# Two-layer GLA and Mamba-2 trunk on one core: squares and gate rows at the start, root and stores at the end, given to other engines and memories

## The chip, the core and the metric

One NeuronCore of a Trainium2 chip. Its engines run side by side and meet at semaphores: TensorE (PE; its weight loads are shown as PEld), VectorE (DVE), ScalarE (ACT), GpSimd (POOL), and SyncE (SP), which here only issues DMAs. The metric is the device time of one execution in microseconds (us); lower is better.

## The reference

The input `x` has 1024 tokens of width 1024, all in float32. Two layers, each with a residual:

```python
for i in range(2):
    hn = rmsnorm(x, norm_w[i])
    x = x + (gla_mixer if i % 2 == 0 else ssd_mixer)(hn, ...)
return rmsnorm(x, final_norm)

def rmsnorm(x, w):
    return x * rsqrt(mean(x * x, -1) + 1e-6) * w
```

The GLA mixer projects `hn` to q, k, v, a gate g and a low-rank decay input `gk_low` (16 columns), runs a chunked recurrence for 4 heads, normalizes each head, multiplies with silu(g) and projects back. The Mamba-2 mixer projects to z, x, B, C and dt, runs a short convolution, a chunked scan for 32 heads in 8 groups, a gated norm, and projects back.

## The kernel before

Activations lie feature-major: eight blocks of 128 features (`KB`) on the partitions, tokens along the free dimension in two tiles of `T = 512`. The four stages in time are GLA on token tile 0, GLA on tile 1, Mamba-2 on tile 0, Mamba-2 on tile 1. float32 products run as three products of rounded parts (`mm3`, lines 223 to 225): high times high, low times high, high times low. So each operand has a high part (`hh`, `wh`, a rounded copy by ScalarE) and a low part (`hl`, `wl`, the difference, by VectorE or GpSimd).

Weights come through a list of `units`. `prefetch` (lines 161 to 188) keeps `RAWS = 3` raw loads and `SPLIT = 4` split weights ahead: the load on SP's queue, line 171 the rounded copy on ScalarE, line 176 the low part on GpSimd. `run` goes through the units and lets generators (the mixers, norms and loads) take steps beside them. The order of the instructions on each engine is not the one in which they are written: a planner in the build puts them in order by readiness in its own model of time and by priority. Exceptions are instructions wrapped in `VP`, `AP_`, `GP` (`InOrder`, line 391), which stay behind everything that was written before them on their engine.

**The start.** `load_acc` brings the eight blocks of `x` into `accs`. `raw_rows` (line 362) makes, for each block k, `hh` = x times the norm weight, rounded (line 370, ScalarE), and `hl` (line 371, VectorE), then squares x (`square_into`, lines 315 to 321: ScalarE into a tile of the pool `t`, VectorE adds it to `ss`). The norm's factor isn't in these rows: the root is made later and multiplied into the results. When the sum `ss` is complete, lines 377 to 388 sum it over partitions on TensorE (lines 379 and 381), take Ln and Exp on ScalarE, and one Newton step on VectorE (`newton`, lines 308 to 313). The first results, q, k and one block of g in three of the four PSUM banks `pp`, can be evicted only with this root (lines 444 and 419). The v products (lines 469 to 471) take all four banks `pp`, so they wait for these evictions. After v comes the small projection `gk` (`small_units`, line 245): its right-hand rows are rebuilt from `hh` + `hl` at line 260, even blocks on VectorE, odd ones on GpSimd, and its matmuls are at line 268. The pool `t` has eight tiles, and PSUM has four banks `pp` and four `mb`.

**The end.** The last output projection of Mamba-2 on tile 1 is done in two halves of 256 tokens, `outp_half(0)` and `outp_half(1)` (line 1120 on): eight blocks of 12 matmuls each; each block is evicted into `accs` by VectorE, squared by ScalarE, and the squares of the second half are added by GpSimd. `final_half(hf)` (line 1162) sums the squares over partitions (line 1168), makes the root (`v`, Ln, Exp, `newton`), scales the eight blocks and stores them in four DMAs of two blocks each. `final_half(0)` runs step by step beside the matmuls of `outp_half(1)`; `final_half(1)` runs alone after the last matmul. Most of these instructions go through the wrapper at line 398, so the rows of the profile name that line.

Of the kernel before, what the change touches and what calls it, by code (L numbers as in the profile page):

```python
# [13 lines left out]
AF = mybir.ActivationFunctionType  # L14
ALU = mybir.AluOpType
# [5 lines left out]
KB = D // P  # L21
# [18 lines left out]
C_NORM = 0  # L40
C_FIN = C_NORM + 16
# [12 lines left out]
def hybrid_kernel(ctx: ExitStack, tc: tile.TileContext, xT, w_in0, w_gk, w_up, w_out0,  # L54
                  w_in1, w_dt, w_out1, par, masks, tri, out):
    nc = tc.nc
    V, A, G, PE = nc.vector, nc.scalar, nc.gpsimd, nc.tensor
    dma = nc.sync.dma_start
# [12 lines left out]
    def tl(tag, bufs, shape=(P, T), dt=F32):  # L71
        cnt[0] += 1
        return sb.tile(list(shape), dt, name=f"{tag}_{cnt[0]}", tag=tag, bufs=bufs)

    def ps(tag):
        cnt[0] += 1
        return (psp if tag == "pp" else psm).tile([P, T], F32, name=f"{tag}_{cnt[0]}", tag=tag)

    def tmp(n=P):
        t = tl("t", NTMP)  # L80
        return t[:] if n == P else t[0:n, :]

    def c3(ap, w=P):
        return ap.rearrange("p (n w) -> p n w", w=w)
# [5 lines left out]
    def act(out, in_, func, **k):  # L90
        name = SILU if func == AF.Silu else LN_EXP
        i = None
        if name != table[0]:
            i = A.preload_act_table_set(name)
            for m in table[2]:
                tc.add_manual_dep(i.ins, m.ins.name, ORDER, reason="table")
            table[:] = name, i, []
        o = A.activation(out, in_, func, **k)
        tc.add_manual_dep(o.ins, table[1].ins.name, ORDER, reason="table")
        table[2].append(o)  # L100
        return o
# [32 lines left out]
    def col(c, n=P):  # L134
        return pr[0:n, c:c + 1]
# [76 lines left out]
    def drain(g):  # L212
        for _ in g:
            pass
# [27 lines left out]

        return [(piece(*src, hf), T, half(hf)) for hf in range(2)]

    def small_units(src, rh, rl, evac):

        box, first = [], len(units)  # L250

        def half(hf):
            def prep():
                if hf == 0:
                    box.append(tl("w2", 1, (P, KB, 32)))
                    A.copy(box[0][:], c3(raws[first][:, 0:KB * 32], 32))
                rows = []
                for k in range(4 * hf, 4 * hf + 4):
                    rows.append(tmp())
                    (G if k % 2 else V).tensor_tensor(rows[-1], rh[k].bitcast(F32), rl[k].bitcast(F32), op=ALU.add)  # L260
                return rows

            def f(*rows):
                if hf == 0:
                    box.append(ps("pp"))
                w, o = box
                for j in range(4):
                    PE.matmul(o[32 * j:32 * (j + 1), :], w[:, 4 * hf + j, :], rows[j], start=(hf == 0), stop=(hf == 1))
                if hf == 1:
                    def sums():  # L270
                        a = tmp(32)
                        A.copy(a, o[0:32, :])
                        for j in range(1, 4):
                            V.tensor_tensor(a, o[32 * j:32 * (j + 1), :], a, op=ALU.add)
                        evac(a)
                    pend.append(sums)
            return f, prep

        for hf in range(2):
            f, prep = half(hf)  # L280
            units.append((None if hf else (src, None), KB * 32, f, None, prep))
# [15 lines left out]
    def rstd_of(p, n, box, var, stay=False):  # L297
        v = tmp() if var is None else var
        V.tensor_scalar(v, p[:], 1.0 / n, EPS, op0=ALU.mult, op1=ALU.add)
        r = p[:] if stay else tl("rstd", 3)[:]  # L300
        l = tmp()
        act(l, v, AF.Ln)
        act(l, l, AF.Exp, scale=-0.5)
        newton(V, r, v, l)
        box.append(r)
        yield

    def newton(eng, r, v, l):

        m = tmp()[:, 0:v.shape[1]]  # L310
        eng.tensor_tensor(m, v, l, op=ALU.mult)
        eng.scalar_tensor_tensor(m, m, -0.5, l, op0=ALU.mult, op1=ALU.mult)
        eng.scalar_tensor_tensor(r, m, 1.5, l, op0=ALU.add, op1=ALU.mult)

    def square_into(ss, src, first, eng):
        if first:
            A.activation(ss, src, AF.Square)
        else:
            sq = tmp()
            A.activation(sq, src, AF.Square)  # L320
            eng.tensor_tensor(ss, ss, sq, op=ALU.add)  # L321
# [38 lines left out]
    accs = {}  # L360

    def raw_rows(rh, rl, r):

        ss = tl("ss", 3)[:]
        for k in range(KB):
            x = accs[k]
            w = col(C_NORM + k)
            a = tl(f"hh{k}", 1, dt=F32R)[:]
            b = tl(f"hl{k}", 1, dt=F32R)[:]
            A.mul(a, x, w)  # L370
            V.scalar_tensor_tensor(b, x, w, a.bitcast(F32), op0=ALU.mult, op1=ALU.subtract)  # L371
            rh.append(a)
            rl.append(b)
            yield
            square_into(ss, x, k == 0, V)
            yield
        with tc.high_priority():
            p, q = ps("mb"), ps("mb")
            PE.matmul(p[:], ones[:], ss, start=True, stop=True)
            for c in range(NC):  # L380
                PE.matmul(q[:, c:c + 1], ss[:, c * P:(c + 1) * P], one, start=True, stop=True)
            drain(rstd_of(p, D, r, None))
            rt = cst.tile([P, 3, NC], F32, name="rtok")
            V.tensor_scalar(rt[:, 0, :], q[:, 0:NC], 1.0 / D, EPS, op0=ALU.mult, op1=ALU.add)
            act(rt[:, 1, :], rt[:, 0, :], AF.Ln)
            act(rt[:, 1, :], rt[:, 1, :], AF.Exp, scale=-0.5)
            newton(V, rt[:, 2, :], rt[:, 0, :], rt[:, 1, :])
        r.append(rt[:, 2, :])
        yield
# [10 lines left out]
    VP, AP_, GP = InOrder(V), InOrder(A), InOrder(G)  # L400


    def load_acc(t):
        for k in range(KB):
            accs[k] = tl(f"acc{k}", 1)[:]
            dma(accs[k], xsrc(0, k, t))
            yield

    class Gla:
# [13 lines left out]
        def gk(self):  # L423
            def evac(o):

                low = o
                if self.raw:
                    V.tensor_tensor(low, o, self.r[0][0:32, :], op=ALU.mult)
                st = tl("stp", 2, (P, T), F32R)
                G.memset(st[96:P, :].bitcast(F32), 0.0)  # L430
                V.tensor_copy(st[0:32, :], low)
                V.tensor_tensor(st[32:64, :], low, st[0:32, :].bitcast(F32), op=ALU.subtract)
                V.tensor_copy(st[64:96, :], low)
                self.low = st[:]
            small_units(w_gk, self.rh, self.rl, evac)

        def qkv(self, h):
            base = h * 10
# [313 lines left out]
    class Ssd:  # L752
# [409 lines left out]
        def final_half(self, hf):  # L1162
            if hf == 0:
                yield
            ts = slice(hf * 256, (hf + 1) * 256)
            p = ps("mb")[:, 0:256]
            for i in (0, KB - 2, KB - 1) if hf else (0, KB - 1):
                PE.matmul(p, ones[:], self.sq[hf][i], start=(i == 0), stop=(i == KB - 1))
            ot = [c3(tl(*(("wh", 5) if hf else ("v", 6)))[:], 256) for _ in range(4)]
            o = [ot[fb // 2][:, fb % 2, :] for fb in range(KB)]  # L1170
            dst = out[:, :, self.t * T + hf * 256:self.t * T + (hf + 1) * 256].rearrange("f p w -> p f w")
            for fb in range(5, KB):
                AP_.mul(o[fb], accs[fb][:, ts], col(C_FIN + fb))
            yield
            v, r, l = tmp()[:, 0:256], tl("rstd", 3)[:, 0:256], tmp()[:, 0:256]
            VP.scalar_tensor_tensor(v, p, 1.0 / D, self.var[:, ts], op0=ALU.mult, op1=ALU.add)
            tc.keep_in_program_order(act(l, v, AF.Ln))
            tc.keep_in_program_order(act(l, l, AF.Exp, scale=-0.5))
            yield
            newton(VP, r, v, l)  # L1180
            yield
            for fb in range(5, KB):
                GP.tensor_tensor(o[fb], o[fb], r, op=ALU.mult)
            for fb in range(5):
                VP.scalar_tensor_tensor(o[fb], accs[fb][:, ts], col(C_FIN + fb), r, op0=ALU.mult, op1=ALU.mult)
                if fb == 1:
                    yield
            for i in range(4):
                dma(dst[:, 2 * i:2 * i + 2, :], ot[i])


    ph = [Gla(0), Gla(1), Ssd(0), Ssd(1)]
# [46 lines left out]
    for p in range(2):  # L1239
        g = ph[p]  # L1240
        for h in range(GH):
            o = [lambda: g.outp(h - 1)] if h else ([lambda: ph[0].outp(3)] if p else [])
# [52 lines left out]
    xs, rows = load_acc(0), raw_rows(ph[0].rh, ph[0].rl, ph[0].r)  # L1295
# [109 lines left out]
```

## Time and profile before

| | us |
|---|---|
| median of 3 runs | 1612.12 (1608.9 to 1615.64) |
| profiled execution, device time | 1609.57 |
| its span, first to last instruction | 1607.8 |
| TensorE busy in the span | 1570.2 (98%) |
| VectorE / ScalarE / GpSimd busy | 951.4 / 951.4 / 655.3 |

The profile is of one execution. A row of a view names an engine, a source line and the tiles in the form written<-read. "waits" are idle stretches of an engine, put down to the instruction that ended last before the engine went on. The chain of waits starts at the last instruction of the span and follows back what released each step. The granted clock is TensorE's, as a share of its full speed.

### The profile page before, as it was taken

To read this page: it belongs to the slowest core of one execution; us is meant where nothing else is said; L and a number is where in the kernel's file an instruction comes from. 1 tells how busy PE (TensorE), PEld (TensorE's weight loads), DVE (VectorE), ACT (ScalarE), POOL (GpSimd) and SP (SyncE) were. 2 spreads that over 40 slices of the span, in tenths; PEclk is the share of its full clock that TensorE was granted. 3 is DMA by queue.
4 is the path that set the end of the run, shared out by engine and by line. 5 is a ranking of instruction groups with operands and counts; after the bars stand their busy time and mean duration, and the time that the engine had idled before them with its cause. 6 is when DMAs were issued, how large, how long until landed. Compare 5 with 4: busy or idle time off the path is not lost.

```text
span 1607.8 us, 24028 instructions
## 1 busy us (share of the span) xinstructions
PE 1570.2 (98%) x8272; PEld 1305.0 (81%) x8272; DVE 951.4 (59%) x1579; ACT 951.4 (59%) x1796; POOL 655.3 (41%) x542
## 2 busy tenths in 40 slices
PE   7999899999999999999999999999999999999996
PEld 5787787878888888888888888888778888888886
DVE  6357567495725446386735544457976963355657
ACT  4445363544636264564865767656657777667743
POOL 6456565643411021216536656565523222222322
PEclk9999999999999999999999999999999999999999
DMA  7545465464576456464586565566665766655752
GB/s 235 194 146 156 137 195 190 132 220 161 183 268 197 151 191 202 154 200 146 174 276 202 179 199 184 181 193 222 226 198 193 240 238 217 206 177 188 259 199 85
DMA packets 172747, 309.30 MB, mean 192 GB/s; under 512 B 19089, under 2 KB 25105, under 8 KB 172625
## 3 DMA queue, kind: packets, MB, share of 16 engines
q1 hardware_dynamic: 172624, 307.77, 58.6%
q8 instruction: 65, 1.06, 0.3%
q14 instruction: 58, 0.47, 0.1%
HBM read 232.06 MB, written 75.63 MB: 191 GB/s over the span
## 4 chain that ended last, share of the span: by engine, by line
PE 78%; DVE 11%; DMA 4%; ACT 4%; issue 1%; POOL 1%; SPq 0%; DVEq 0%; ACTq 0%; POOLq 0%
PE pp L223 18%; PE pp L224 18%; PE pp L225 18%; PE pp L469 3%; PE pp L470 3%; PE pp L471 3%; DMA wraw<-w_in 2%; PE mb L956 2%; PE mb L709 2%; PE mb L708 2%; PE mb L658 1%; PE mb L949 1%; DVE o L604 1%; PE mb L223 1%; PE mb L224 1%
## 5 line engine op out<-in xcount | busy, mean ns | idle before, releaser
L171 ACT CAST wh<-wraw 128x512 fp32r<-128x512 f32 x472 | 289.4, 618 | 343.1 <-PE pp L224 164.3
L223 PE MATMUL pp<-hh,wh 128*128 128x512 f32 x1184 | 468.5, 397 | 8.8 <-ACT wh L171 7.4
L224 PE MATMUL pp<-hl,wh 128*128 128x512 f32 x1184 | 464.0, 392 | 1.3 <-DVE hl L371 1.1
L225 PE MATMUL pp<-hh,wl 128*128 128x512 f32 x1184 | 463.0, 392 | 0.0
L176 POOL TENSOR_TENSOR wl<-wraw,wh 128x512 fp32r<-128x512 f32 x240 | 328.3, 1375 | 277.1 <-ACT wh L171 232.3
L223 PEld LDWEIGHTS pp<-hh,wh 128*128 128x128 f32 x1184 | 222.8, 188 | 60.3 <-ACT wh L171 9.0
L224 PEld LDWEIGHTS pp<-hl,wh 128*128 128x128 f32 x1184 | 223.0, 188 | 48.5 <-DVE hl L371 2.5
L225 PEld LDWEIGHTS pp<-hh,wl 128*128 128x128 f32 x1184 | 222.9, 188 | 46.2
L223 PE MATMUL pp<-yh,wh 128*128 128x512 f32 x448 | 177.9, 397 | 6.1 <-DVE acc L515 5.4
L225 PE MATMUL pp<-yh,wl 128*128 128x512 f32 x448 | 175.9, 393 | 0.0
L224 PE MATMUL pp<-yl,wh 128*128 128x512 f32 x448 | 175.4, 392 | 0.0
L321 POOL TENSOR_TENSOR ss<-ss,t 128x512 f32<-128x512 f32 x53 | 74.0, 1396 | 81.8 <-ACT t L320 70.4
L223 PEld LDWEIGHTS pp<-yh,wh 128*128 128x128 f32 x448 | 84.2, 188 | 26.1 <-issue 2.8
L469 PE MATMUL pp<-wh,hh 128*128 128x512 f32 x256 | 100.4, 394 | 2.7 <-DVE m L444 2.7
L470 PE MATMUL pp<-wl,hh 128*128 128x512 f32 x256 | 100.3, 392 | 0.0
L471 PE MATMUL pp<-wh,hl 128*128 128x512 f32 x256 | 99.7, 392 | 0.0
L225 PEld LDWEIGHTS pp<-yh,wl 128*128 128x128 f32 x448 | 84.3, 188 | 18.9 <-issue 0.2
L224 PEld LDWEIGHTS pp<-yl,wh 128*128 128x128 f32 x448 | 84.2, 188 | 17.8
L827 DVE SCALAR_TENSOR_TENSOR m<-pp,pr,m 128x509 f32<-128x509 f32 (+2 forms) x96 | 70.4, 743 | 42.8 <-ACT m L824 41.7
L827 DVE SCALAR_TENSOR_TENSOR x<-pp,pr,x 128x509 f32<-128x509 f32 (+2 forms) x96 | 71.2, 743 | 32.5 <-ACT x L824 31.4
L648 POOL TENSOR_TENSOR t<-v,t 128x512 fp32r<-128x512 f32 x28 | 38.1, 1371 | 112.6 <-DMA wraw<-w_in 28.9
L1038 POOL TENSOR_TENSOR t<-t,o 128x512 fp32r<-128x512 f32 x32 | 41.8, 1310 | 91.6 <-ACT o L1036 87.0
(286 smaller groups left out, 2623.7 us busy)
## 6 DMA issues: line engine op xcount, KB each, us to landing
wraw<-w_in SPq DMA_DIRECT2D x352, 256.0 KB, 3.5
low_in<-wl SPq DMA_DIRECT2D x176, 256.0 KB, 3.8
wl<-low_in SPq DMA_DIRECT2D x176, 256.0 KB, 3.2
wraw<-w_out SPq DMA_DIRECT2D x128, 256.0 KB, 3.5
low_out<-wl SPq DMA_DIRECT2D x64, 256.0 KB, 4.0
v<-a_cum SPq DMA_DIRECT2D x64, 256.0 KB, 3.8
wl<-low_out SPq DMA_DIRECT2D x56, 256.0 KB, 3.2
xn<-x SPq DMA_DIRECT2D x43, 256.0 KB, 3.8
```

What stands on the lines that cost most here:

```text
L171: A.copy(hi[:, 0:w], raws[n][:, 0:w])
L176: G.tensor_tensor(lo[:, 0:w], raws[n][:, 0:w], hi[:, 0:w].bitcast(F32), op=ALU.subtract)
L223: PE.matmul(o, lh, rh, start=first, stop=False)
L224: PE.matmul(o, lh, rl, start=False, stop=False)
L225: PE.matmul(o, ll, rh, start=False, stop=last)
L321: eng.tensor_tensor(ss, ss, sq, op=ALU.add)
L469: PE.matmul(o, rh[kb][:, cs], wh[:], start=(kb == 0), stop=False)
L470: PE.matmul(o, rh[kb][:, cs], wl[:], start=False, stop=False)
L471: PE.matmul(o, rl[kb][:, cs], wh[:], start=False, stop=(kb == KB - 1))
L648: G.tensor_tensor(vl, v[c], vh.bitcast(F32), op=ALU.subtract)
L827: V.scalar_tensor_tensor(dst[:, s:], o[:, 0:T - s], col(C_CW + j * 32 + si), dst[:, s:], op0=ALU.mult, op1=ALU.add)
L1038: G.tensor_tensor(xel[-1], xe, hi.bitcast(F32), op=ALU.subtract)
```

## The change

- In `raw_rows` the square of block 0 is pinned in ScalarE's order behind what was written before it; those of blocks 1 to 7 go to a PSUM bank of the tag `mb` instead of a tile of the pool `t`, and VectorE adds them from there.
- In `small_units`, for the first GLA stage only, the eight rows are made by ScalarE as `accs[k]` times the norm weight instead of by VectorE and GpSimd as `hh` + `hl`.
- In `final_half` the result of the Newton step stays in the PSUM bank `p` of the sum. ScalarE copies it to SBUF for GpSimd. GpSimd scales blocks 6 and 7 (ScalarE multiplies their column factor in ahead) instead of 5 to 7, and VectorE scales 0 to 5, reading the root from PSUM.
- In the second half, the stores of the pairs 1 and 3 are issued from ScalarE's queue, those of 0 and 2 from SP's.

```diff
--- before.py
+++ after.py
@@ -242,7 +242,7 @@
 
         return [(piece(*src, hf), T, half(hf)) for hf in range(2)]
 
-    def small_units(src, rh, rl, evac):
+    def small_units(src, rh, rl, evac, again=None):
 
 
 
@@ -257,6 +257,9 @@
                 rows = []
                 for k in range(4 * hf, 4 * hf + 4):
                     rows.append(tmp())
+                    if again:
+                        again(k, rows[-1])
+                        continue
                     (G if k % 2 else V).tensor_tensor(rows[-1], rh[k].bitcast(F32), rl[k].bitcast(F32), op=ALU.add)
                 return rows
 
@@ -372,7 +375,13 @@
             rh.append(a)
             rl.append(b)
             yield
-            square_into(ss, x, k == 0, V)
+            if k == 0:
+
+                AP_.activation(ss, x, AF.Square)
+            else:
+                sq = ps("mb")[:]
+                A.activation(sq, x, AF.Square)
+                V.tensor_tensor(ss, sq, ss, op=ALU.add)
             yield
         with tc.high_priority():
             p, q = ps("mb"), ps("mb")
@@ -432,7 +441,8 @@
                 V.tensor_tensor(st[32:64, :], low, st[0:32, :].bitcast(F32), op=ALU.subtract)
                 V.tensor_copy(st[64:96, :], low)
                 self.low = st[:]
-            small_units(w_gk, self.rh, self.rl, evac)
+            small_units(w_gk, self.rh, self.rl, evac,
+                        (lambda k, row: A.mul(row, accs[k], col(C_NORM + k))) if self.raw else None)
 
         def qkv(self, h):
             base = h * 10
@@ -1169,24 +1179,26 @@
             ot = [c3(tl(*(("wh", 5) if hf else ("v", 6)))[:], 256) for _ in range(4)]
             o = [ot[fb // 2][:, fb % 2, :] for fb in range(KB)]
             dst = out[:, :, self.t * T + hf * 256:self.t * T + (hf + 1) * 256].rearrange("f p w -> p f w")
-            for fb in range(5, KB):
+            for fb in range(6, KB):
                 AP_.mul(o[fb], accs[fb][:, ts], col(C_FIN + fb))
             yield
+
             v, r, l = tmp()[:, 0:256], tl("rstd", 3)[:, 0:256], tmp()[:, 0:256]
             VP.scalar_tensor_tensor(v, p, 1.0 / D, self.var[:, ts], op0=ALU.mult, op1=ALU.add)
             tc.keep_in_program_order(act(l, v, AF.Ln))
             tc.keep_in_program_order(act(l, l, AF.Exp, scale=-0.5))
             yield
-            newton(VP, r, v, l)
-            yield
-            for fb in range(5, KB):
+            newton(VP, p, v, l)
+            yield
+            AP_.copy(r, p)
+            for fb in range(6, KB):
                 GP.tensor_tensor(o[fb], o[fb], r, op=ALU.mult)
-            for fb in range(5):
-                VP.scalar_tensor_tensor(o[fb], accs[fb][:, ts], col(C_FIN + fb), r, op0=ALU.mult, op1=ALU.mult)
+            for fb in range(6):
+                VP.scalar_tensor_tensor(o[fb], accs[fb][:, ts], col(C_FIN + fb), p, op0=ALU.mult, op1=ALU.mult)
                 if fb == 1:
                     yield
             for i in range(4):
-                dma(dst[:, 2 * i:2 * i + 2, :], ot[i])
+                (AP_.dma_start if hf and i % 2 else dma)(dst[:, 2 * i:2 * i + 2, :], ot[i])
 
 
     ph = [Gla(0), Gla(1), Ssd(0), Ssd(1)]
```

## Rows read from the trace of the kernel before

**Rows 1.** The page: busy us, share of the span, instructions.
```profile
PE 1570.2 (98%) x8272; PEld 1305.0 (81%) x8272; DVE 951.4 (59%) x1579; ACT 951.4 (59%) x1796; POOL 655.3 (41%) x542
```

**Rows 2.** Windows: length, busy (count) PE, PEld, DVE, ACT, POOL; clock, DMA share, GB/s.
```profile
23.66:32.75 9.09, 9.09 (x41) 7.22 (x40) 8.16 (x11) 3.26 (x7) 8.07 (x6) 1.00 0.72 226
32.75:35.43 2.68, 0.00 (x2) 0.00 (x1) 2.68 (x6) 0.12 (x1) 1.38 (x2) 1.00 0.85 287
35.43:40.50 5.07, 5.07 (x15) 4.04 (x16) 1.74 (x3) 0.50 (x1) 3.88 (x4) 0.66 0.30 99
```

**Rows 3.** Waits, 0 to 60 us: total us, times, longest.
```profile
PE pp L469 <- DVE m L444: 2.7, 1, 2.7
...
PE mb L379 <- DVE ss L321: 0.5, 1, 0.5
```

**Rows 4.** Chain of waits, 0 to 62 us: start, us, what.
```profile
20.06 1.77 DVE ss L321
...
29.39 2.30 DVE t L260 x2
...
32.30 1.68 DVE t L260
...
34.72 0.66 DVE m L444
```

**Rows 5.** Timeline, GpSimd, 19 to 60 us: start, us, instruction.
```profile
24.81 2.55 POOL L260 TENSOR_TENSOR t<-hh,hl 128x512 f32<-128x512 f32 x2
```

**Rows 6.** Single lines: ns min/median/max, first and last start.
```profile
L321 DVE TENSOR_TENSOR ss<-ss,t x35: 672/692/1793, 10.4 to 1265.9; 128x512 f32<-128x512 f32 x35
...
L889 DVE TENSOR_TENSOR acc<-pp,acc x40: 672/683/693, 1023.6 to 1575.2; 128x512 f32<-128x512 f32 x40
```

**Rows 7.** Groups by form, ScalarE: busy us, mean ns, idle before.
```profile
L722 ACT COPY o<-mb 128x256 f32<-128x256 f32 x32 | 12.0, 374 | 45.0 <-PE mb L709 45.0
...
L370 ACT ACTIVATE hh<-acc,pr 128x512 fp32r<-128x512 f32 x8 | 5.7, 714 | 2.2 <-DMA acc<-xT 2.2
...
L553 ACT COPY mb<-m 128x512 f32<-128x512 f32 x8 | 4.7, 591 | 8.3 <-DVE m L551 8.3
```

**Rows 8.** Chain of waits, 1594 to 1608 us.
```profile
1594.82 0.73 POOL ss L398
...
1595.60 1.58 PE mb L1168 x6
```

**Rows 9.** Timeline, 1585 to 1608 us, of single engines.
```profile
1584.96 0.59 PE L1168 MATMUL mb<-ss,ones 128*128 128x256 f32 x2
...
1589.35 0.74 POOL L398 TENSOR_TENSOR v<-v,rstd 128x256 f32<-128x256 f32 x1 [0.43 <-DVE rstd L398]
...
1590.90 0.28 PE L225 MATMUL mb<-ktok,hl 128*128 128x256 f32 x1
...
1591.51 2.38 DVE L398 SCALAR_TENSOR_TENSOR v<-acc,pr,rstd 128x256 f32<-128x256 f32 x3
...
1593.73 0.28 PE L225 MATMUL mb<-ktok,hl 128*128 128x256 f32 x1
...
1594.48 0.41 DVE L398 TENSOR_TENSOR acc<-mb,acc 128x256 f32<-128x256 f32 x1
...
1600.01 3.47 DVE L398 SCALAR_TENSOR_TENSOR wh<-acc,pr,rstd 128x256 f32<-128x256 f32 x5
```

**Rows 10.** Stores: SP's issues; DMA busy tenths and GB/s, 1601 to 1607.8, 40 slices.
```profile
1603.11 0.89 SPq L1189 DMA_DIRECT2D out<-wh  x2
...
1604.09 0.45 SPq L1189 DMA_DIRECT2D out<-wh  x1
...
DMA  0000000399991000029999999999999300000000
GB/s 0 0 0 0 0 0 0 120 361 337 355 319 48 0 0 0 0 78 331 319 349 374 320 313 379 343 350 331 355 355 319 109 0 0 0 0 0 0 0 0
```

**Rows 11.** Windows, behind the start (columns as in rows 2).
```profile
57.50:200.00 142.50, 136.42 (x750) 113.25 (x750) 89.54 (x167) 66.84 (x124) 77.43 (x61) 1.00 0.48 151
```

## Prediction

> **What bounds the kernel now.** I read the page first: TensorE is busy 1570.2 of 1607.8 us [rows 1], so everything between the two ends is a full TensorE, and a change at the ends can win only the 37.6 us in which it stands still. [...] The view of waits names the causes: 2.7 us for the eviction `m` (line 444), 0.5 us for the sum of squares `ss` (line 321) [rows 3]. The chain of waits then shows what made these late. The last add into `ss` took 1.77 us, and ahead of the eviction at 34.72 VectorE spent 2.30 and 1.68 us on line 260, the adds that rebuild the rows for the small gate projection [rows 4], which nobody needs before 57 us. While VectorE waited there, GpSimd ran its own half of these adds and the weight splits [rows 5].
>
> At the other end the last product starts at 1593.73, and from there to 1607.8 runs one serial chain: the late eviction, squares, GpSimd's last add, six matmuls of the cross-partition sum, root, scaling, stores [rows 8, 9]. After the last issue (1604.09) three stores are still in flight back to back at some 340 GB/s with the DMA engines over 90% busy [rows 10].
>
> **The start, part by part.** *Squares in PSUM.* Seven adds `ss` keep their place and count; one operand now comes from PSUM. With two SBUF operands this add takes 672 ns at best and 1793 at worst; with a PSUM operand the same shape took 672 to 693 in all 40 cases [rows 6], though GpSimd is busy for 41% of the span [rows 1]. So the last add falls from 1.77 to 0.69, 1.1 us sooner. TensorE gets only the part in which it stood: 0.5 us [rows 3], since its queue is full up to there. The last `hl` (line 371, two SBUF operands) keeps its collision with GpSimd, so the gap ahead of it stays. ScalarE's square into PSUM is not in the trace; the nearest row is a copy of the same shape into PSUM, 591 ns [rows 7], so I take 0.6, unchanged. The four banks `mb` turn over fast enough: the fifth square needs the bank of the first, whose add is by then over 2 us old.
>
> [...]
>
> *First square pinned.* It moves behind the first weight cast on ScalarE; the first product could start some 0.5 us sooner. That is lost later in the wait for the last `hl`: zero. If it doesn't come, nothing is lost either. A clock that rises sooner would be a gain that I don't count.
>
> *Rows by ScalarE.* Four adds leave VectorE and four leave GpSimd (2.55 us for one pair [rows 5]); eight scalings of a 128x512 tile come to ScalarE, at 714 ns each by line 370, the same form: 5.7 us. ScalarE is busy only 3.26 of 9.09 us from 23.66 to 32.75, 0.12 of 2.68 and 0.50 of 5.07 behind that [rows 2], so they fit there; what waits behind them in its queue are weight casts, which run several units ahead. Ahead of the eviction 4.0 us of VectorE's work go (2.30 and 1.68 [rows 4]), plus the 0.5 from `ss`: the eviction starts near 30.2 and ends near 30.9, while TensorE would run out of banks at 32.75 less 0.5. The 2.68 us go entirely, with 1.3 us to spare. What is late next is the eviction of the third bank, two operations of 0.7 us behind: it just fits.
>
> *The clock.* The stretch of 5.07 us at 0.66 lost 0.34 x 5.07 = 1.7 us, right after the gap. Without the gap I count this as won.
>
> Sum at the start: 0.5 + 2.7 + 1.7 = 4.9. Against it: three of the eight row tiles may be free from the beginning (no square draws from their pool any more), and their scalings need only the input. A planner could put them ahead of the first operands on ScalarE, where there is little room. Each costs 0.71; three are 2.1, and the lower end is zero, if they fall into ScalarE's waits for weights. I take 0.4, nearer to zero, since the other five have the room of the windows. Start: **4.5**, between 1.5 and 5.5. From 57 us on TensorE is the limit again and the 4.5 us stay.
>
> **The end, part by part.** *VectorE's backlog.* In the first half's scaling three operations took 2.38 us (0.79 each), so the evictions of blocks 5 to 7 queued up and the last began at 1594.48, though the products of block 5 were done at 1591.2 and those of block 7 at 1594.0 [rows 9]. The root now lies in PSUM; the eviction with a PSUM operand in the same rows takes 0.41, and I take 0.43 with the column factor. The four scalings that stand behind the eviction of block 4 then take 1.7 us instead of three in 2.4. The last eviction follows its product at 1594.1 instead of 1594.48: 0.4 us. More is won in the sum: block 5's square and GpSimd's add (0.73, ended at 1595.55 [rows 8]) now end near 1594.1, so the first four of the six matmuls (1.58 us in all [rows 8]) run while the last square is made. Only two, 0.59 us [rows 9], stand behind it: 1594.1 + 0.41 + 0.45 + 0.05 + 0.59 gives 1595.6 instead of 1597.17: **1.55**.
>
> The copy of the root for GpSimd is new: ScalarE, PSUM to SBUF at 128x256, 374 ns [rows 7]. In the first half it waits for the root, and behind it in the queue is the square of block 4, whose eviction comes later anyway. GpSimd starts 0.4 to 0.8 us later but has two products instead of three (0.74 each uncontended), and its last add still ends at about 1594.1: cover just complete. If it fails, each 0.1 us late there is 0.1 at the end.
>
> *The last scaling and the stores.* Root to last scaling was 3.47 us for five operations, 0.69 each instead of some 0.43 [rows 9], beside three products of GpSimd. Six at 0.44 are 2.6. GpSimd's two end at 0.45 + 2 x 0.74 = 1.95 after the root, ahead of that. The last pair of blocks can be stored 2.6 us after the root instead of 3.5, and nothing is behind it. Before, the last issue stood at 4.1 (1604.09 - 1600.01), and three transfers of 0.77 us each (768 KB at 340 GB/s) ended at 6.3 [rows 10]. Now the pairs are issued at 0.9 (SP), 1.8 (ScalarE), 2.15 (ScalarE) and 2.6 (SP). An issue reaches the wire 0.8 us later (issued at 1603.11, the row of slices of 0.17 us fills again from 1603.9); the three late ones take the wire from 2.6 to 4.9. So 6.3 becomes 4.9: **1.4**. With SP alone, the fourth issue would stand at 3.05 and its data end at 5.0: the second queue itself is worth only 0.1. A ScalarE issue is not in the trace; SP's cost some 0.45 [rows 10]. I take the same; if it were a microsecond slower, 0.5 of the gain goes, while a faster one wins nothing, as the wire is full.
>
> [...]
>
> End: **3.0**, between 1.4 and 3.5.
>
> **Rivals.** (a) *The head's gain is taken back.* The rows on ScalarE stand in front of first operands or of the exponentials of the root, or the eviction meets another wait; the gap shrinks but the clock falls all the same. Against it stands 1.3 us of room, for it that nothing in the trace shows the new order. Then the end's 3.0 and some 0.6 remain: 1608.5. (b) *A PSUM operand doesn't free VectorE* in operations with a column factor, so the change does not do what it says. Against it are the 40 even durations [rows 6]. The end then keeps 0.5, the start its 3 to 4 us, as the removed adds are gone in any case: 1608. (c) *Slower.* The order on each engine is planned at build; a shifted head re-plans the first layer's mixers, where TensorE stands 6.1 us between 57.5 and 200 [rows 11]. If the new order doubled this and a half-clock stretch (1.7) followed at two of the gaps, 9.5 us would be lost: 1614. It decides against the change from 7.5 us on. Nothing in the profile speaks for it except that these gaps hang on VectorE's order.
>
> **How the numbers follow.** 4.5 + 3.0 = 7.5 us. The profiled execution took 1609.57, its span 1607.8 and 1.8 around it; it would become 1602.1. The median of the three runs is 2.55 above the profiled one, so on that scale 1612.12 - 7.5 = **1604.6**. Half a per cent, about what a measurement of this kernel can tell from no change, is 8.1 us (1604.06), just beyond the forecast. Forecast 0.57, (a) 0.21, (b) 0.06, (c) 0.06, and 0.10 for a new order that wins more than I counted (a clock that rises sooner, half of the waits of 57 to 200: 3 us more, 1601.6). Of the forecast's 0.57 I give 0.29 to less than 8.1 us and 0.28 to more. That makes 0.28 + 0.10 = 0.38 faster; 0.29, 0.21, 0.06 and 0.02 of (c) = 0.58 the same; 0.04 slower, if (c) costs more than its price. The range goes from the upper bounds (5.5 + 3.5 = 9.0 and 3 us of scatter, as the runs show 1608.9 to 1615.6) to rival (a) with 2 us of scatter: 1600 to 1610.5.
>
> **What would show it.** Right: no gap over 0.5 us ahead of the products of line 469, full clock from 32 to 41, `ss` adds all near 0.69, the small projection's matmuls at about 53 instead of 57.5, the last evictions within 0.1 us of their products, scalings at 0.43, the last store issued about 1601. Wrong: row scalings on ScalarE before 18 us with later `hh`; a new gap ahead of line 469 or a low clock there; six matmuls still behind GpSimd's last add; an issue on ScalarE well over 0.5 us; more TensorE idle time between 57 and 200 than the 6.1 us of now.

## The result, and the profile after

The change made the kernel a little faster. Six executions of each on one chip:

| | before | after |
|---|---|---|
| median, us | 1611.46 (1608.9 to 1615.64) | 1602.09 (1601.37 to 1604.0) |
| ratio after / before | | 0.9944 (95% interval 0.9933 to 0.9955) |
| profiled execution: device time, span | 1609.57, 1607.8 | 1601.62, 1599.8 |

The median fell by 9.4 us, the profiled span by 8.0. The span splits at two marks that both traces have: the first matmul of the small projection, and the start of the last product (the last of the three matmuls of the last block).

| | before | after | gain |
|---|---|---|---|
| to the small projection | 57.46 | 51.62 | 5.84 |
| from there to the last product | 1536.27 | 1535.88 | 0.39 |
| last product to the end (the tail) | 14.07 | 12.30 | 1.77 |

So the start gave more than the 4.5 that were forecast, the end less than the 3.0. By the prediction's own line of 8.1 us the median's 9.4 count as faster, to which it had given 0.38.

**The start.** Windows of the kernel after, columns as in [rows 2]:

```profile
23.66:32.75 9.09, 8.49 (x38) 6.70 (x38) 6.57 (x13) 7.40 (x14) 4.43 (x5) 1.00 0.90 285
32.75:35.43 2.68, 2.68 (x13) 2.19 (x12) 0.03 (x1) 1.25 (x3) 1.87 (x2) 1.00 0.44 114
35.43:40.50 5.07, 5.07 (x24) 4.20 (x23) 0.00 (x0) 1.93 (x4) 3.29 (x3) 1.00 0.69 240
...
57.50:200.00 142.50, 137.69 (x736) 115.83 (x735) 87.32 (x164) 66.16 (x122) 77.51 (x62) 0.98 0.48 147
```

The window that was empty in [rows 2] is full, and the one behind it has the full clock. What is left of the waits of [rows 3] (waits of TensorE, 0 to 60 us):

```profile
PE pp L223 <- ACT wh L171: 7.5, 1, 7.5
PE pp L479 <- DVE m L454: 0.6, 1, 0.6
```

The wait for the sum of squares is gone, and 0.6 of the 2.7 us for the eviction are left. All seven adds of squares (line 384) take the same time, where [rows 6] had them up to 1793 ns:

```profile
L384 DVE TENSOR_TENSOR ss<-mb,ss x7: 676/678/679, 10.6 to 20.5; 128x512 f32<-128x512 f32 x7
```

The new order is read from the timeline of single engines, 19 to 60 us:

```profile
25.82 0.62 ACT L171 CAST wh<-wraw 128x512 fp32r<-128x512 f32 x1 [1.11 <-DMA wraw<-w_in]
26.34 0.62 ACT L98 ACTIVATE t<-t 128x512 f32<-128x512 f32 x1
...
27.00 1.35 DVE L314 TENSOR_TENSOR t<-t,t 128x512 f32<-128x512 f32 x1 [2.22 <-ACT t L98]
...
27.96 3.17 ACT L445 ACTIVATE t<-acc,pr 128x512 f32<-128x512 f32 x5
...
28.84 0.39 PE L479 MATMUL pp<-wh,hh 128*128 128x512 f32 x1
...
30.89 0.69 DVE L454 SCALAR_TENSOR_TENSOR m<-pp,rstd 128x512 f32<-128x512 f32 x1
```

The row scalings (line 445) run late and close together, as ScalarE has nothing else to do there. The v products begin at 28.84 instead of 31.00, the eviction at 30.89 instead of 34.68. And a new wait is to be seen: the root's exponential stands on ScalarE behind a weight cast that waits 1.11 us for its DMA, and VectorE idles 2.22 us for it.

**Behind the start.** The last row of the windows above has a granted clock of 0.98 where [rows 11] has 1.00. Two stretches at half clock stand there, from 155.1 and from 165.3 us on, 3.4 us each; the kernel before has none in that window. The window of the second one, then the matmuls behind the wait at that place, first after, then before:

```profile
165.30:168.70 3.40, 2.90 (x26) 2.91 (x28) 3.33 (x11) 0.00 (x0) 0.00 (x0) 0.50 0.76 263
```

```profile
165.80 2.40 PE L668 MATMUL mb<-raw,m 128*64 128x160 f32 x16 [2.72 <-DVE raw L614]
171.63 1.31 PE L658 MATMUL mb<-raw,m 128*64 128x160 f32 x16 [2.96 <-DVE raw L604]
```

Up to this wait the kernel after is 5.83 us ahead; the 16 matmuls behind it then take 2.40 us instead of 1.31, so 1.1 us of the start's gain is lost at once. The wait itself was there before, and longer (2.96 us), without a half clock. In gp_root, gp_root_timed and sq5_in_sum the clock from 57.5 to 200 us is 1.00.

**The tail.** Timeline of the kernel after, engines side by side:

```profile
1582.14 0.85 DVE L407 SCALAR_TENSOR_TENSOR mb<-t,t 128x256 f32<-128x256 f32 x1
...
1583.67 0.35 ACT L407 COPY rstd<-mb 128x256 f32<-128x256 f32 x1
1584.06 0.87 DVE L407 SCALAR_TENSOR_TENSOR v<-acc,pr,mb 128x256 f32<-128x256 f32 x2 [0.74 <-ACT rstd L407]
...
1587.50 0.28 PE L225 MATMUL mb<-ktok,hl 128*128 128x256 f32 x1
...
1587.76 0.73 POOL L407 TENSOR_TENSOR ss<-ss,t 128x256 f32<-128x256 f32 x1 [0.70 <-ACT t L407]
1587.82 0.42 DVE L407 TENSOR_TENSOR acc<-mb,acc 128x256 f32<-128x256 f32 x1 [0.32 <-PE mb L225]
...
1588.54 0.70 PE L1178 MATMUL mb<-ss,ones 128*128 128x256 f32 x2 [0.76 <-POOL ss L407]
1589.08 1.03 PE L1178 MATMUL mb<-t,ones 128*128 128x256 f32 x4
...
1592.96 0.37 ACT L407 COPY rstd<-mb 128x256 f32<-128x256 f32 x1 [1.42 <-DVE mb L407]
1593.37 2.44 DVE L407 SCALAR_TENSOR_TENSOR wh<-acc,pr,mb 128x256 f32<-128x256 f32 x6 [0.44 <-ACT rstd L407]
...
1595.05 0.98 ACTq L407 DMA_DIRECT2D out<-wh  x2
```

VectorE's backlog is gone: the last eviction starts 0.04 us behind its product (0.28 us from 1587.50), and six scalings take 2.44 us where [rows 9] had 3.47 for five. But in both halves VectorE's first scaling waits for ScalarE's copy of the root (0.74 and 0.44 us), and GpSimd's last add still releases the six matmuls of the sum, 0.76 us late.

### The profile page after: what moved, and what is told of

Its sections match the earlier page's. It is cut to its first block, busy times and chain, and to the rows that moved or that the text cites. A ratio compares the mean times of both kernels' runs of the same rounds, so it can differ in the third digit from the quotient of the medians.

```text
span 1599.8 us, 24024 instructions
## 1 busy us (share of the span) xinstructions
PE 1569.5 (98%) x8272; PEld 1306.2 (82%) x8272; DVE 942.5 (59%) x1577; ACT 956.7 (60%) x1804; POOL 646.6 (40%) x536
## 4 chain that ended last, share of the span: by engine, by line
PE 82%; DVE 9%; ACT 3%; DMA 3%; issue 1%; POOL 1%; SPq 0%; DVEq 0%; POOLq 0%; ACTq 0%
PE pp L223 19%; PE pp L225 19%; PE pp L224 19%; PE pp L479 3%; PE pp L480 3%; PE pp L481 3%; PE mb L966 2%; PE mb L719 2%; PE mb L718 2%; DMA wraw<-w_in 1%; PE mb L668 1%; PE mb L959 1%; DVE o L614 1%; PE mb L223 1%; PE mb L224 1%
```

## The experiments

Two theories stood for the start. *Rows:* moving the eight rows takes the gap and the half clock away, and the squares bring the v products forward. *One part alone:* the rows do it all, or the squares do. For the tail: either ScalarE's copy holds VectorE, or only GpSimd's lag counts. Ratios are to the kernel before, on the same chip.

| run | ratio (95% interval) | small projection | tail |
|---|---|---|---|
| start_only | 0.9958 (0.9945 to 0.9972) | 52.47 | 14.09 |
| end_only | 0.9988 (0.9974 to 1.0003) | 57.51 | 12.32 |
| rows_only | 0.9992 (0.9972 to 1.0013) | 52.95 | 14.11 |
| squares_only | 1.0014 (1.0000 to 1.0028) | 59.73 | 14.00 |
| after_again | 0.9949 (0.9931 to 0.9967) | 51.98 | 12.26 |
| gp_root_timed | 0.9932 (0.9919 to 0.9945) | 51.49 | 11.38 |
| gp_root_sq5 | 0.9932 (0.9920 to 0.9944) | 51.51 | 11.34 |
| gp_root, sq5_in_sum, root_sbuf, one_queue, no_pin | one execution each | 51.78, 51.50, 51.78, 51.78, 51.17 | 11.34, 11.76, 13.62, 12.21, 12.29 |

**start_only.** The function `final_half` of the kernel before in the kernel after.

> The start of the change alone; the end as before. Theory (the ends add up): the small projection's matmuls begin at 51.6 us as in the full change (57.5 before), the last product of the last half is some 6 us earlier than before, and the tail from that product to the end is 14.1 us as before: 6 us faster in all, ratio 0.996. Rival (the order of the middle is re-planned by the end's code, or the shift is lost in the first layer's mixers): under 4 us.

The tail is that of before, and the small projection begins 5.0 us sooner (52.47; 51.6 was expected). By the ratio the kernel is 6.8 us faster (0.9958), so the first theory holds: the start's gain lives on to the end. The one trace shows less: the last product starts at 1589.91, only 3.8 us earlier than before, where some 6 were expected.

**end_only.** `final_half` of the kernel after; the squares and the rows as before.

> The end of the change alone; the start as before. Theory: the start keeps its 2.7 us gap and its stretch at half clock, the tail from the last product's start to the end of the span is 12.3 us as in the full change instead of 14.1: 1.8 us faster. Rival (the tail gained 3 us as forecast, and something else in the full change took 1.2 back): 3 us faster.

The tail is 12.32, the gap of 2.7 us stays. The timed gain, some 1.9 us by the ratio, agrees, though its interval reaches 1.0003. The two ends together, 0.9958 and 0.9988, make 0.9946: they add up to what the whole change gave.

**rows_only.**

```diff
-            if k == 0:
-                AP_.activation(ss, x, AF.Square)
-            else:
-                sq = ps("mb")[:]
-                A.activation(sq, x, AF.Square)
-                V.tensor_tensor(ss, sq, ss, op=ALU.add)
+            square_into(ss, x, k == 0, V)
```

and `final_half` as before.

> Only the eight rows for the small projection made by ScalarE; squares in SBUF and the end as before. Theory (the rows carry the eviction, the squares carry the order of the products): the gap before line 469's products falls from 2.7 to under 1 us and no half clock follows, but these products begin near 30.5, not 28.8; the small projection begins at 53 to 53.5. Rival (the rows alone change the planner's order of the products too): 51.6 to 52.

Waits of TensorE, 0 to 60 us, and rows of the timeline of single engines:

```profile
PE pp L224 <- DVE hl L374: 1.2, 2, 0.9
PE mb L382 <- DVE ss L324: 0.5, 1, 0.5
```

```profile
28.07 0.69 DVE L448 SCALAR_TENSOR_TENSOR m<-pp,rstd 128x512 f32<-128x512 f32 x1
...
31.10 0.39 PE L473 MATMUL pp<-wh,hh 128*128 128x512 f32 x1
```

The v products begin where they did before (31.10 against 31.00), the eviction is 3 us ahead of them, no wait for it is left, and the clock stays full from 23.66 to 40.50. The small projection begins at 52.95, 4.5 us sooner: 2.7 of the gap and 1.7 of the clock, and hardly anything else. That is the forecast's mechanism by itself, to 0.1 us. The timed ratio is another matter: 0.9992 with an interval from 0.9972 to 1.0013, executions from 1605 to 1619 us and a single one of 9011, which the ratio leaves out. The profiled one took 1605.33 and had, like the kernel after, a clock of 0.98 from 57.5 to 200 us. Whether the gain of the start is lost later in the others, no trace shows; it stays open.

**squares_only.** The rows at line 260 and `final_half` as before.

```diff
-                    if again:
-                        again(k, rows[-1])
-                        continue
```

> Only the squares in PSUM and the pinned first square; the rows on VectorE and GpSimd and the end as before. Theory (squares carry the order): the v products begin near 29 instead of 31.0, but then wait 3 to 4 us for the eviction, with a half clock behind, so the small projection begins at 56 to 57. Rival (the squares win the collisions only, the order stays): v products at 30.5, the gap stays 2.7, 57.0.

Waits of TensorE, 0 to 62 us, then windows:

```profile
PE pp L476 <- DVE m L451: 3.7, 1, 3.7
PE pp L477 <- POOL wl L176: 2.4, 1, 2.4
```

```profile
35.43:40.50 5.07, 2.80 (x7) 2.22 (x8) 4.63 (x7) 0.00 (x0) 4.20 (x4) 0.54 0.77 239
40.50:46.00 5.50, 5.50 (x21) 4.45 (x20) 0.00 (x0) 0.00 (x0) 0.00 (x0) 0.80 0.00 0
```

The v products begin at 28.84, as in the whole change: the squares (here with the pin) carry this. But the rows still stand on VectorE and GpSimd; TensorE waits 2.4 and 3.7 us, the clock is low for longer (0.54 and 0.80 in two windows), and the small projection begins at 59.73, 2.3 us later than before. I expected 56 to 57: I had not counted that GpSimd's two rows also hold the weight splits. Alone, this half of the change costs time at the start; the timed ratio can't tell it from no change (1.0014, the interval begins at 1.0000). The whole change gets 1.3 us more than rows_only (51.62 against 52.95) out of it: 2.3 us sooner, less the 0.6 us of the eviction wait that comes back and 0.3 that no wait accounts for.

**no_pin.**

```diff
-                AP_.activation(ss, x, AF.Square)
+                A.activation(ss, x, AF.Square)
```

> The full change without the pin: the square of block 0 may go ahead of the first weight cast again. Theory (the pin is worth nothing, the first product waits for the landing of the weights and the start is limited by the later rows): first v product at 28.8 to 29.2 and small projection at 51.5 to 52 as with the pin. Rival (the pin carries the sooner products): v products at 30 or later.

The v products begin at 29.32, 0.1 us later than the upper end I gave (29.2), and the small projection at 51.17, sooner than in the other kernels with the full start and the pin (51.49 to 51.98). The pin is not what brings the v products forward, as the theory said. But it is not without a price. Rows of no_pin's timeline:

```profile
23.46 0.63 ACT L98 ACTIVATE t<-t 128x512 f32<-128x512 f32 x1
...
25.82 0.62 ACT L171 CAST wh<-wraw 128x512 fp32r<-128x512 f32 x1 [1.63 <-DMA wraw<-w_in]
...
27.94 0.68 DVE L454 SCALAR_TENSOR_TENSOR m<-pp,rstd 128x512 f32<-128x512 f32 x1
```

Without the pin the root's exponential stands ahead of the weight cast that waits for its DMA, where the kernel after has it behind. The eviction starts at 27.94 instead of 30.89, and TensorE has no wait for it any more. In all ten runs with the pin the exponential stands behind that cast, in the four without (before, end_only, rows_only, no_pin) ahead of it. So the 0.6 us of wait that the change left came with the pin: without it the v products begin 0.5 us later, and the small projection still 0.45 us sooner. How the pin of an early square moves the exponential in the planner's order, no run shows, and the one execution (1602.52 us) says nothing on the whole.

The first product of all began at 6.62 to 7.66 us in the runs of this study, with the pin and without; in gp_root and gp_root_timed, one program, at 6.62 and 7.52. In all of them it waits for the first weight cast; in the kernel after, that cast waits 1.05 us for its load and the product begins at 7.51.

**gp_root and gp_root_timed.** One kernel in two runs, with one execution and with six. GpSimd makes its own root in SBUF, so that ScalarE doesn't touch the bank (`newton` returns its term `m`; `c15` is a column of 1.5).

```diff
-            newton(VP, p, v, l)
-            yield
-            AP_.copy(r, p)
+            m = newton(VP, p, v, l)
+            AP_.activation(v, m, AF.Identity, bias=c15[:, 0:1])
+            GP.tensor_tensor(r, v, l, op=ALU.mult)
+            yield
```

> The full change, but GpSimd makes its own copy of the root from SBUF (ScalarE adds 1.5 to the Newton term beside VectorE's last step, GpSimd multiplies), so that ScalarE no longer reads the bank in which the root lies. Theory (VectorE is held by ScalarE's copy, since two engines read one PSUM tile): the first scaling starts within 0.1 us of the root in both halves instead of 0.44 and 1.1 us behind it, GpSimd's last add ends before the last product, and the tail falls from 12.3 to about 11.1 us. Rival (the copy holds only GpSimd): the tail stays within 0.3 us of 12.3.

> The kernel of gp_root again, timed beside the full change on one chip. Theory (the tail's 1.0 us is all that differs, the middle is scatter): ratio to before 0.9935 to 0.994, about 0.0006 below that of the full change in the same call; tail 11.3. Rival (the added operations shift the planner's order elsewhere, as the later last product of its one look, 1590.6 against 1587.5, suggests): no faster than the full change, though the tail is 11.3.

Timeline of the tail of gp_root_timed:

```profile
1581.24 0.43 DVE L410 SCALAR_TENSOR_TENSOR mb<-t,t 128x256 f32<-128x256 f32 x1
...
1581.91 0.86 DVE L410 SCALAR_TENSOR_TENSOR v<-acc,pr,mb 128x256 f32<-128x256 f32 x2
...
1586.62 0.28 PE L227 MATMUL mb<-ktok,hl 128*128 128x256 f32 x1
...
1587.03 0.70 PE L1181 MATMUL mb<-ss,ones 128*128 128x256 f32 x2
1587.57 1.05 PE L1181 MATMUL mb<-t,ones 128*128 128x256 f32 x4
...
1591.06 0.43 DVE L410 SCALAR_TENSOR_TENSOR mb<-t,t 128x256 f32<-128x256 f32 x1
...
1591.53 2.44 DVE L410 SCALAR_TENSOR_TENSOR wh<-acc,pr,mb 128x256 f32<-128x256 f32 x6
...
1591.65 0.73 POOL L410 TENSOR_TENSOR rstd<-t,t 128x256 f32<-128x256 f32 x1 [4.67 <-ACT t L410]
```

The first scaling follows the root at once (1591.06 + 0.43 to 1591.53), and the sum's matmuls start 0.41 us behind the start of the last product instead of 1.04. The tail is 11.34 and 11.38 (about 11.1 was expected): 0.9 us less than after. So the copy did hold VectorE, in both halves. Timed beside the full change it has 0.9932 (0.9935 to 0.994 was expected) against 0.9949. The intervals overlap, so the times alone don't separate the two; the tail does. By median it is the best version of this study, level with gp_root_sq5 (1600.7 us against 1601.7 for after_again).

**sq5_in_sum.**

```diff
-            for i in (0, KB - 2, KB - 1) if hf else (0, KB - 1):
+            for i in (0, KB - 3, KB - 2, KB - 1) if hf else (0, KB - 1):
```

and GpSimd adds only up to block 4 in the second half.

> The full change, but the square of block 5 in the second half goes straight into the cross-partition sum (eight matmuls) instead of through GpSimd's last add. Theory (GpSimd's last add releases the sum's matmuls 0.8 us late): the matmuls begin at the last product's end, and though there are two more, the tail falls by about 0.4 to 11.9 us. Rival (the last square is what counts): no change, or 0.4 us more for the two matmuls.

```profile
1587.86 0.59 PE L1178 MATMUL mb<-ss,ones 128*128 128x256 f32 x2
...
1588.29 1.46 PE L1178 MATMUL mb<-t,ones 128*128 128x256 f32 x6
```

These rows of its timeline start 0.12 us behind the start of the last product at 1587.74. The tail is 11.76, 0.5 less in spite of two more matmuls: GpSimd's last add was what the sum waited for.

**gp_root_sq5.** Both edits.

> Both mends of the tail: GpSimd's own root, and block 5's square straight into the sum. Theory (behind the last product the chain of the last square ends last once GpSimd is early): the matmuls of the sum end 2.0 us behind the last product's start as in gp_root, so the tail is 11.2 to 11.4 and nothing is won over gp_root. Rival (the two mends add up): 10.8.

Tail 11.34, as in gp_root: the two mends are for one and the same delay. What ends last now would be the last square and the matmuls behind it, as the theory has it; no run takes these two apart.

**root_sbuf.** The root in SBUF, read there by VectorE and GpSimd, no copy; all else as after.

```diff
-            newton(VP, p, v, l)
+            newton(VP, r, v, l)
             yield
-            AP_.copy(r, p)
```

> The full change, but the root goes to SBUF as before and all engines read it there; no copy; the split of six blocks and two, and the two queues, stay. Theory (a PSUM operand frees VectorE of GpSimd's hold): no wait for a copy (0.45 us less), but the scalings that run beside GpSimd's two products take 0.8 to 0.9 us instead of 0.41, six of them about 3.3 us instead of 2.4; tail 12.5 to 12.9. Rival (where the root lies doesn't matter): tail 11.9.

Rows of its timeline:

```profile
1583.21 1.79 DVE L407 SCALAR_TENSOR_TENSOR v<-acc,pr,rstd 128x256 f32<-128x256 f32 x2
...
1585.26 2.29 DVE L407 SCALAR_TENSOR_TENSOR v<-acc,pr,rstd 128x256 f32<-128x256 f32 x4
...
1593.67 3.40 DVE L407 SCALAR_TENSOR_TENSOR wh<-acc,pr,rstd 128x256 f32<-128x256 f32 x6
1593.80 1.79 POOL L407 TENSOR_TENSOR wh<-wh,rstd 128x256 f32<-128x256 f32 x2 [4.60 <-DVE rstd L407]
```

Six scalings take 3.40 instead of 2.44 us, and in the first half the six take 1.79 + 2.29 instead of 0.87 + 1.65. The tail is 13.62, longer than I expected, because the first half loses as well and its evictions are late again. Against gp_root, which has no copy either, the place of the root is worth 2.3 us.

**one_queue.** All four last stores by SP.

```diff
-                (AP_.dma_start if hf and i % 2 else dma)(dst[:, 2 * i:2 * i + 2, :], ot[i])
+                dma(dst[:, 2 * i:2 * i + 2, :], ot[i])
```

> The full change, but all four last stores issued by SP. Theory (the wire is full, the queue saves issue time only): the tail is 12.3 to 12.5 us. Rival (the second queue carries the gain of the stores): 12.8 or more.

The tail is 12.21 against 12.30 and 12.26 with two queues: the second queue wins nothing.

**after_again.** The kernel after, unchanged.

> The full change once more, as the measure for the run beside it: ratio to before 0.994 to 0.9955, tail 12.3, small projection at 51.5 to 52, first product between 7.0 and 7.7 us, which follows the landing of the first weights and not the order.

It did as the first time: tail 12.26, small projection at 51.98.

## Why the prediction was right, and where it was not

The time (1602.09 us) lies 2.5 us below the forecast of 1604.6 and within the range. That the sum is so near is luck in part: the start gave 1.3 us more than its 4.5, the end 1.2 less than its 3.0, and the two errors cancel. Part of the difference is the scale: on its span the forecast was 7.5 us and the span gave 8.0, while the medians lie 9.4 apart, as the profiled execution of before was a quick one.

*Right, with its size.* The gap at the eviction and the half clock behind it: 4.4 us forecast, 4.5 measured in rows_only, by these two alone. The PSUM operand: adds at 678 ns each, against 672 at best with two SBUF operands [rows 6]; scalings at 0.41 instead of the 0.43 I took; root_sbuf shows what happens without it. ScalarE's square into PSUM: 0.58 for the 0.6 taken. The second queue: 0.1 forecast, nothing measured. The scaling and the stores: from VectorE's first scaling to the end 1.36 us were won of the 1.4 (7.79 before, 6.43 after). Rival (b) did not come. Of (a), the half clock behind the gap did not come.

*Rivals that came in part.* Of (a), the root's exponential did come late, behind a weight cast, at 0.6 us. Of (c), the half clock in the first layer's mixers came: 1.1 us at least, behind the wait at 165.8. That TensorE's idle time between 57.5 and 200 fell from 6.1 to 4.8 us speaks neither for nor against it, as at half clock the same matmuls keep TensorE busy for longer (16 of them 2.40 us against 1.31): in gp_root, with a clock of 1.00 there, it is 6.1 again. In the profiled execution the loss is regained further on, in the part that scatters (0.39 us were won over the whole middle).

*The squares' term was mis-sized.* I gave TensorE the 0.5 us in which it stood for `ss`, "since its queue is full up to there", and left the gap ahead of the last `hl`. The planner put the products in another order instead, as far as the rows can tell: TensorE no longer stands ahead of the last `hl` (1.1 us in two waits before) nor ahead of the sum (0.5), and does other products there. It was busy for 8.85 of the 10.46 us from 13.20 to 23.66 before, now for 10.27:

```profile
13.20:23.66 10.46, 8.85 (x40) 6.13 (x38) 10.39 (x15) 6.17 (x12) 5.27 (x4) 1.00 0.70 239
13.20:23.66 10.46, 10.27 (x47) 7.58 (x45) 9.42 (x14) 6.36 (x12) 5.47 (x4) 1.00 0.77 264
```

The v products came 2.2 us sooner. squares_only shows that the squares do this, and no_pin that it doesn't take the pin. The gain that the prediction named and didn't count, a clock that rises sooner, isn't needed for it: the granted clock is 1.00 from 7.00 to 23.66 us before and after alike. Single matmuls, 0.63 to 0.80 us at first, came down to 0.39 us by 13.6 us before and by 12.0 after, but in after_again by 13.7, and there the v products began at 28.69 all the same. But the eviction came at 30.89, not near the 30.2 of the prediction, and was needed sooner. So the "1.3 us to spare" were not there: 0.6 us of the wait remain, by ScalarE's weight cast ahead of the exponential, and no_pin shows that this order came with the pin, which I had put at zero. Net, squares and pin gave 1.3 us over rows_only; the squares without the pin gave 1.8 (51.17).

*The early rows were mis-sized.* I took 0.4 off for row scalings ahead of the first operands. None stands before 27.96: zero.

*The step that failed is the copy of the root.* I wrote that it delays GpSimd only, and let VectorE scale at once. But VectorE's first scaling waits for ScalarE's copy (its row in the tail names `rstd`, which it doesn't read), although both only read the bank. That cost 0.44 us in the second half; in the first half the copy itself stood behind a square on ScalarE, so it cost 0.74 there, and that pushed evictions, squares and GpSimd's last add until the "cover just complete" was gone: the sum began 1.04 us behind the start of the last product instead of 0.4. Forecast 3.0, measured 1.8; without the copy (gp_root) 2.7. By terms, from the start of the last product: the end of the sum's matmuls was to come 1.55 us sooner than before (3.44), and came 0.83 sooner (2.61); in gp_root_timed, where they start 0.41 us behind as forecast, 1.44 (2.00). What is left to 3.0 is small: 0.1 here, 0.1 in the scaling and stores, the remainder in rounding and the steps between.

## What to carry to other kernels

Where VectorE and GpSimd work side by side, keep one operand of VectorE's in PSUM: here that made scalings of 0.41 us out of the 0.57 to 0.9 of root_sbuf. But let only one engine read that bank on the path that ends last: as this kernel was built, a copy for another engine from the same bank was a wait for both (0.44 and 0.74 us), and making that root from what lies in SBUF took 0.9 us off the tail.

A part of a change that feeds the bottleneck sooner can cost time by itself: the squares and the pin alone made the small projection 2.3 us later, and paid only once the work that stood ahead of the eviction had been moved. And an instruction that is pinned in its order moves others: one that was costed at zero put the exponential behind a weight cast.

## What was not expected of the hardware

One program's trace can differ from execution to execution by more than the effects that are hunted here: gp_root and gp_root_timed are the same kernel, and from the small projection to the last product they took 1538.78 and 1535.13 us. The last product of gp_root:

```profile
1590.56 0.28 PE L227 MATMUL mb<-ktok,hl 128*128 128x256 f32 x1
```

The granted clock shows two places where it arose. Two windows, first of gp_root, then of gp_root_timed:

```profile
898.20:901.60 3.40, 3.40 (x12) 2.90 (x11) 2.57 (x6) 2.14 (x5) 2.51 (x2) 0.50 0.72 217
1266.90:1270.30 3.40, 3.40 (x14) 3.08 (x13) 3.29 (x6) 0.93 (x2) 0.19 (x1) 0.50 0.85 307
898.20:901.60 3.40, 3.40 (x18) 2.87 (x17) 2.92 (x4) 0.95 (x2) 1.90 (x2) 1.00 0.84 210
1266.90:1270.30 3.40, 3.40 (x19) 2.79 (x18) 3.40 (x7) 3.37 (x6) 0.00 (x0) 1.00 0.17 60
```

In gp_root TensorE stood 1.9 us for an operand from ScalarE ahead of the first window and 2.0 us ahead of the second, and the clock was at half behind both; in gp_root_timed it did not stand in the first place and 1.0 us in the second, and the clock stayed full. By the prediction's price, half of the stretch, the two cost 1.7 us each, and the waits themselves are 1.9 and 1.0 us longer. That is more than the 3.65 us; where the rest was won back, no row here shows. Why the waits came in one execution and not in the other stays open, and the count of such stretches isn't everything: the kernel after has three between the two marks and a clock of 0.98 from 57.5 to 200 us, after_again has 0.99 there, and they took 1535.88 and 1537.26 us.

The two ends, on the other hand, repeat to 0.1 us (tails of 14.07, 14.09, 14.11 and 14.00 with `final_half` of before). So the ends were judged by their own stretches, and the whole by medians.
